# A seven-product block MLP for the second half of the tokens, and the sample's tokens in block 1

## The chip, the cores and the metric

The kernel runs on one core of a Trainium2 chip, as one program. The metric is the device time of one execution in microseconds, from runs on the chip. The engines of the core are named as the profile names them: PE (TensorE, matrix products), DVE (VectorE), ACT (ScalarE), POOL (GpSimd) and SP (SyncE, which here issues every DMA).

## The reference, cut to what matters

One layer of a streaming encoder is computed for a prompt of 2048 tokens and a sample of 32 tokens behind a cache of 128, with a model width of 1024:

```python
qa, ka, va, qb, kb, vb = split_proj(rmsnorm(h, g_attn), w_in)       # 1024 -> 3072
oa = differential attention, 4 heads, chunk-causal, T5 bias          # group A
ob = attention in a band of 9 chunks of 64, 8 heads, clipped bias    # group B
h = h + merge(oa, ob) @ w_out                                        # 1024 -> 1024
c = rmsnorm(h, g_mlp)
h = h + jnp.square(jax.nn.relu(c @ w_up)) @ w_down                   # 1024 -> 4096 -> 1024
h = h + jax.nn.sigmoid(h @ w_ple_gate) * (p @ w_ple_proj)
y = rmsnorm(h, g_final)
```

The outputs are y for prompt and sample and the new keys and values. All is in fp32.

## The kernel before

**Data.** Activations lie transposed: 128 partitions of channels, tokens along the free axis. The tokens are cut into four blocks, of 512, 512, 512 and 544 columns; the last block holds the 32 sample tokens. `SUBS` says in which column runs a block goes through a matrix product: one run of 512, and for the block of 544 two of 272. The residual h, the queries, keys, values and attention outputs are kept in DRAM between stages.

**Products.** Each fp32 operand is split into a high part, rounded to the matmul's format, and a low remainder. `split` (L167) has ACT make the high part and POOL (or DVE) the low part by a subtraction; POOL works in pieces of 256 columns (`pool_tt`, L148). `mm3` (L187) computes one product by three matmuls: high x high, high x low, low x high. A weight tile comes through `wunit` (L178): DMA of the raw tile (two buffers), high and low part (three buffers each).

**Stages.** `run` (L1105) prepares and projects blocks 0 and 1, then alternates attention over pairs of query tiles with projections of further blocks: group A's first half (`JA0`), group B's first half, group B's second half, group A's second half (`JA1`). The sample counts as pair 8, in the last tuple of `JA1` and `JB`; `caches` (L469) brings the cached keys and values into the scratch tensors ahead of block 3's projection. Then come output projection, MLP, gate and final norm. Blocks 0 and 1 go through the MLP one at a time, with two PSUM banks (`mm`), while the other six belong to attention. After that attention's banks go to a pool `md`: output projections of 2 and 3, gate and final of block 0, and then the MLP of blocks 2 and 3 together.

**The MLP** (`mlp`, L982) takes 256 of the 4096 hidden channels at a time: `mlp_up` (L922) multiplies two weight tiles by the normed activations (8 channel tiles, 24 matmuls a run), ACT applies relu and square, and the result is split; `mlp_down` (L950) multiplies it by two tiles of w_down for each of 8 output tiles (6 matmuls a run), and DVE adds each PSUM result to h in SBUF (L980). So the down sum over 4096 channels is made in SBUF, in 16 additions for each output.

**Order.** The order of instructions on each engine and of the DMAs on SP's queue is laid down when the program is compiled: a planner goes through a simulated time line, takes ready instructions by their place in the program, and hands out the buffers of the pools as they come free. `weave` and `weave2` interleave two stages by hand, `drain` runs one to its end. On the chip each engine and SP follows its list in order and waits by semaphores.

## Time and profile before

| | |
|---|---|
| runs (3) | 3239.21 us median, 3234.81 to 3240.3 |
| span of the profiled execution, first to last instruction | 3235.4 us |
| mean granted PE clock | 0.983 |
| PE / DVE / ACT / POOL busy | 3075.5 / 1568.3 / 1693.0 / 1715.2 us |
| matmuls | 17881 |
| DMA traffic | 489 MB, 151 GB/s over the span |

The profile gives no time of its own for the profiled execution beside the span; the difference of the median to the span is 3.8 us. Busy times overlap between engines, so they do not add up to the span. A PE time of one instruction overlaps that of the next; the pace of matmuls is read from their starts.

### The profile page before, as it was taken

What the parts mean: (1) busy time and instruction counts of PE and PEld (TensorE: products, weight loads), DVE (VectorE), ACT (ScalarE), POOL (GpSimd) and SP (SyncE); (2) the same over time, 40 slices, a digit from 0 to 9 for tenths busy, and PEclk for the clock granted to TensorE, in tenths of its full rate; (3) what the DMA queues carried; (4) which work ended last, traced back from release to release, by engine and by line L of the source; (5) the groups of instructions that cost most, each with busy time, mean ns of one, the idle gap of its engine ahead of it and who ended that gap; (6) DMA issues with size and microseconds to landing.
All of it is one profiled execution on the core that took longest, in us unless ns stands there. A gap on an engine that the chain in (4) does not pass through costs nothing.

```text
span 3235.4 us, 51443 instructions
## 1 busy us (share of the span) xinstructions
PE 3075.5 (95%) x17881; PEld 2690.7 (83%) x17881; DVE 1568.3 (48%) x3952; ACT 1693.0 (52%) x3717; POOL 1715.2 (53%) x2515
## 2 busy tenths in 40 slices
...
GB/s 233 156 256 247 227 246 212 197 255 212 209 235 226 207 144 135 157 162 140 183 136 153 148 114 121 130 131 271 146 100 46 47 46 46 46 46 46 50 94 89
DMA packets 519084, 489.02 MB, mean 151 GB/s; under 512 B 37884, under 2 KB 414016, under 8 KB 518824
## 3 DMA queue, kind: packets, MB, share of 16 engines
...
q8 instruction: 142, 2.33, 0.3%
q14 instruction: 118, 0.97, 0.1%
HBM read 379.06 MB, written 110.49 MB: 151 GB/s over the span
## 4 chain that ended last, share of the span: by engine, by line
PE 54%; DVE 5%; DMA 4%; ACT 2%; issue 1%; POOL 1%; SPq 0%; DVEq 0%; POOLq 0%; ACTq 0%
PE ups L191 7%; PE dps L191 7%; PE ups L192 7%; PE ups L193 7%; PE dps L192 7%; PE dps L193 7%; PE s L572 2%; PE gps L191 1%; PE gps L192 1%; PE gps L193 1%; DMA wr<-w_down 1%; PE tpp L644 1%; DVE e L609 1%; PE ob L771 1%; PE o L659 1%
## 5 line engine op out<-in xcount | busy, mean ns | idle before, releaser
L165 POOL TENSOR_TENSOR wl<-wr,wh 128x256 fp32r<-128x256 f32 x936 | 699.0, 780 | 473.4 <-ACT wh L170 448.6
L170 ACT ACTIVATE wh<-wr 128x1024 fp32r<-128x1024 f32 x338 | 357.2, 1058 | 611.4 <-PE dps L192 298.4
L980 DVE TENSOR_TENSOR h<-h,dps 128x512 f32<-128x512 f32 (+1 forms) x640 | 373.1, 585 | 578.4 <-PE dps L193 565.9
L155 POOL TENSOR_TENSOR wl<-wr,wh 128x256 fp32r<-128x256 f32 x416 | 304.3, 764 | 385.7 <-ACT wh L170 380.2
L191 PE MATMUL dps<-uh,wh 128*128 128x512 f32 (+1 forms) x1280 | 457.3, 357 | 16.9 <-DVE h L980 9.3
L191 PE MATMUL ups<-cH,wh 128*128 128x512 f32 (+1 forms) x1280 | 452.4, 354 | 10.0 <-ACT relu L945 8.1
L192 PE MATMUL ups<-cL,wh 128*128 128x512 f32 (+1 forms) x1280 | 451.5, 353 | 0.8 <-POOL cL L155 0.5
L193 PE MATMUL ups<-cH,wl 128*128 128x512 f32 (+1 forms) x1280 | 450.7, 352 | 0.0
L193 PE MATMUL dps<-uh,wl 128*128 128x512 f32 (+1 forms) x1280 | 449.7, 352 | 0.0
L192 PE MATMUL dps<-ul,wh 128*128 128x512 f32 (+1 forms) x1280 | 449.5, 351 | 0.0
L155 POOL TENSOR_TENSOR ul<-relu,uh 128x136 fp32r<-128x136 f32 (+1 forms) x320 | 200.5, 649 | 178.0 <-ACT uh L170 173.7
L191 PEld LDWEIGHTS dps<-uh,wh 128*128 128x128 f32 x1280 | 241.2, 188 | 52.2 <-DVE h L980 15.2
L191 PEld LDWEIGHTS ups<-cH,wh 128*128 128x128 f32 x1280 | 241.1, 189 | 43.6 <-ACT relu L945 8.9
L193 PEld LDWEIGHTS dps<-uh,wl 128*128 128x128 f32 x1280 | 240.8, 188 | 33.2 <-POOL wl L155 0.7
L192 PEld LDWEIGHTS ups<-cL,wh 128*128 128x128 f32 x1280 | 241.8, 189 | 31.5 <-POOL cL L155 0.8
L193 PEld LDWEIGHTS ups<-cH,wl 128*128 128x128 f32 x1280 | 241.4, 189 | 29.7
L192 PEld LDWEIGHTS dps<-ul,wh 128*128 128x128 f32 x1280 | 241.3, 189 | 26.0
L191 PE MATMUL qps<-aH,wh 128*128 128x512 f32 (+1 forms) x640 | 231.1, 361 | 10.0 <-ACT kr L433 3.4
L192 PE MATMUL qps<-aL,wh 128*128 128x512 f32 (+1 forms) x640 | 229.4, 358 | 0.0
L193 PE MATMUL qps<-aH,wl 128*128 128x512 f32 (+1 forms) x640 | 229.3, 358 | 0.0
L586 ACT ACTIVATE e<-s,nm 128x512 f32<-128x512 f32 (+3 forms) x256 | 155.2, 612 | 78.9 <-DVE nm L578 62.5
L572 PE MATMUL s<-ka,q 128*128 128x512 f32 (+3 forms) x768 | 184.0, 341 | 11.1 <-DMA q<-qS 3.7
(220 smaller groups left out, 7095.6 us busy)
## 6 DMA issues: line engine op xcount, KB each, us to landing
...
q<-qS SPq DMA_DIRECT2D x256, 128.0 KB, 4.1
...
```

Of the source, the lines that this page charges most:

```text
L155: nc.gpsimd.tensor_tensor(out[:, sl], a[:, sl], b[:, sl], op=op)
L165: nc.gpsimd.tensor_tensor(out[:, sl], a[:, sl], b[:, sl], op=op)
L170: nc.scalar.activation(hi, raw, AF.Copy)
L191: nc.tensor.matmul(ps, lh, rh, start=start and i == 0, stop=False)
L192: nc.tensor.matmul(ps, lh, rl, start=False, stop=False)
L193: nc.tensor.matmul(ps, ll, rh, start=False, stop=stop and i == n - 1)
L572: nc.tensor.matmul(s, q[:, m, hl, P * qi : P * qi + nr], kt[:, m, k0 - kb : k0 - kb + n], start=hl == 0, stop=hl == 1)
L586: nc.scalar.activation(dst, src, AF.Exp, bias=nmx, accum_out=z[:nr, m, bi : bi + 1])
L609: nc.vector.scalar_tensor_tensor(e[0][:nr, sl], e[0][:nr, sl], c[:nr, 0, bi : bi + 1], e[1][:nr, sl], op0=ALU.mult, op1=ALU.add)
L644: nc.tensor.transpose(tp[:kn, x, :nr], w[:nr, P * i : P * i + kn], self.ident[:nr, :nr])
L659: nc.tensor.matmul(oo, v[:kn, x, 0], pL[:kn, x, q0:nq], start=False, stop=False)
L980: nc.vector.tensor_tensor(hv, hv, ps, op=ALU.add)
```

## The change

**The sample** moves from block 3 to block 1. Block 1 becomes 544 columns in two runs of 272, block 3 becomes 512 in one. Scratch tensors keep the sample's columns behind block 1's (`T0`, `tcol`). The sample's attention becomes part of the second tuple of `JA0` and `JB`, and `caches` is called before all attention.

**The MLP of blocks 2 and 3** becomes two block products of 2 x 2, each by seven products in place of eight. The two token blocks are the two column halves of the right operand; its row halves are channels 0 to 511 and 512 to 1023 (up) and hidden channels 0 to 2047 and 2048 to 4095 (down).

- *Up* (`uphase`, `strassen`): for each of 16 groups of 256 hidden channels, `wquads` loads the weight's four quarters and makes four sums and differences (DVE). Each of seven products is 12 matmuls into one PSUM bank; ACT and DVE combine the products to four outputs; relu and square follow, and the result goes to DRAM (`uS`). The seven right operands are made once: `xnorm` norms, stores to DRAM (`cS`) and splits four of them beside block 0's gate, `xdiff` reads back and makes the three others after `final(0)`.
- *Down* (`dphase`): seven products in turn, each over the whole of a half's 2048 hidden channels in four PSUM banks, 192 matmuls. Both operands of each of 16 steps are formed and split as they are needed (`operand`); raw weights are loaded again for each product, activations once, through 24 buffers. After a product, DVE adds or subtracts its four banks into one or two quarters of h.

**Pools.** From the second half's output projection on, a new pool `tw` holds 5 raw weight buffers, 9 shared operand buffers and a ring of 14 tiles of 512 columns; all eight PSUM banks are one pool. The gate of block 1 uses the two banks `mm` as before.

```diff
 BLK = 544
 SUBS = {
     0: [(0, 512)],
-    1: [(0, 512)],
+    1: [(0, 272), (272, 272)],
     2: [(0, 512)],
-    3: [(0, 272), (272, 272)],
+    3: [(0, 512)],
 }
-BN = {0: 512, 1: 512, 2: 512, 3: 544}
+BN = {0: 512, 1: 544, 2: 512, 3: 512}
+T0 = {0: 0, 1: 512, 2: 1056, 3: 1568}
+TS = 1024
 HALVES = [(0, 1), (2, 3)]
...
-JA0 = [(0, 1), (2, 3)]
-JA1 = [(4, 5), (6, 7, 8)]
-JB = [(0, 1), (2, 3), (4, 5), (6, 7, 8)]
+JA0 = [(0, 1), (2, 3, 8)]
+JA1 = [(4, 5), (6, 7)]
+JB = [(0, 1), (2, 3, 8), (4, 5), (6, 7)]
...
         self.dma(raw, src)
-        hi = self.wp.tile([P] + shape, F32R, tag="wh", bufs=3, name="wh")
-        lo = self.wp.tile([P] + shape, F32R, tag="wl", bufs=3, name="wl")
+        th, tl, n = self.wtags
+        hi = self.wp.tile([P] + shape, F32R, tag=th, bufs=n, name="wh")
+        lo = self.wp.tile([P] + shape, F32R, tag=tl, bufs=n, name="wl")
         self.split(hi, lo, raw, hi_eng, lo_eng)
...
 
+    def quad(self, b, k):
+        return self.cS[:, k, 512 * (b - 2) : 512 * (b - 1)]
+
+    def tsplit(self, dst, src, lo_eng):
+        self.split(dst[:, 0], dst[:, 1], src, "act", lo_eng)
+
+    def xnorm(self, big, big2, t2, wk, out):
+        nc = self.nc
+        r = {}
+        for b in HALVES[1]:
+            r[b] = wk.tile([P, 512], F32, tag="r", bufs=2, name="rl")
+            self.dma(r[b], self.rS[:, T0[b] : T0[b] + 512])
+
+        def normed(b, k):
+            t = t2.tile([P, 512], F32, name="cn")
+            self.dma(t, self.hS[:, k, T0[b] : T0[b] + 512])
+            nc.vector.scalar_tensor_tensor(
+                t, t, self.g_mlp[:, k : k + 1], r[b], op0=ALU.mult, op1=ALU.mult
+            )
+            self.dma(self.quad(b, k), t)
+            return t
+
+        def x(pool, name):
+            out[name] = pool.tile([P, 4, 2, 512], F32R, tag="act", name="X" + name)
+            return out[name]
+
+        b11, b21 = x(big, "b11"), x(big, "b21")
+        for k in range(4):
+            for t, kk in ((b11, k), (b21, 4 + k)):
+                self.tsplit(t[:, k], normed(2, kk), "dve" if kk % 2 else "pool")
+            yield
+        b22, t3 = x(big2, "b22"), x(big2, "t3")
+        for k in range(4):
+            lo, hi = normed(3, k), normed(3, 4 + k)
+            self.tsplit(b22[:, k], hi, "pool")
+            nc.vector.tensor_tensor(lo, hi, lo, op=ALU.subtract)
+            self.tsplit(t3[:, k], lo, "dve")
+            yield
+
+    def xdiff(self, big, t2, out):
+        nc = self.nc
+        t1, tt2, t4 = [big.tile([P, 4, 2, 512], F32R, tag="act", name="X" + n) for n in ("t1", "t2", "t4")]
+        out.update(t1=t1, t2=tt2, t4=t4)
+        for k in range(4):
+            q = {}
+            for n, b, kk in (("12", 3, k), ("11", 2, k), ("22", 3, 4 + k), ("21", 2, 4 + k)):
+                q[n] = t2.tile([P, 512], F32, name="q" + n)
+                self.dma(q[n], self.quad(b, kk))
+            nc.vector.tensor_tensor(q["12"], q["12"], q["11"], op=ALU.subtract)
+            self.tsplit(t1[:, k], q["12"], "pool")
+            nc.vector.tensor_tensor(q["22"], q["22"], q["12"], op=ALU.subtract)
+            self.tsplit(tt2[:, k], q["22"], "dve")
+            nc.vector.tensor_tensor(q["21"], q["22"], q["21"], op=ALU.subtract)
+            self.tsplit(t4[:, k], q["21"], "pool")
+            yield
+
+    def wquads(self, W, c0, t2):
+        nc = self.nc
+        raw = []
+        for j in range(2):
+            r = self.rawp.tile([P, 4, 256], F32, bufs=self.nraw, name="wq")
+            self.dma(r, W[512 * j : 512 * j + 512, c0 : c0 + 256].rearrange("(k p) c -> p k c", p=P))
+            raw.append(r)
+        q = {"11": raw[0][:, :, :P], "12": raw[1][:, :, :P], "21": raw[0][:, :, P:], "22": raw[1][:, :, P:]}
+
+        def comb(n, x, y, op):
+            q[n] = t2.tile([P, 4, P], F32, name="w" + n)
+            nc.vector.tensor_tensor(q[n], q[x], q[y], op=op)
+
+        comb("s1", "21", "22", ALU.add)
+        comb("s2", "s1", "11", ALU.subtract)
+        comb("s3", "11", "21", ALU.subtract)
+        comb("s4", "12", "s2", ALU.subtract)
+        return q
+
+    def wsplit(self, src):
+        w = self.wp.tile([P, 2, 4, P], F32R, tag="wc", bufs=self.wtags[2], name="wc")
+        nc = self.nc
+        nc.scalar.activation(w[:, 0], src, AF.Copy)
+        for i in range(2):
+            sl = slice(2 * i, 2 * i + 2)
+            nc.gpsimd.tensor_tensor(w[:, 1, sl], src[:, sl], w[:, 0, sl].bitcast(F32), op=ALU.subtract)
+        return w
+
+    def prod(self, q, name, x, md):
+        w = self.wsplit(q[name])
+        ps = md.tile([P, 512], F32, tag="mm", name="xps")
+        self.mm3(ps, [(w[:, 0, k], w[:, 1, k], x[:, k, 0], x[:, k, 1]) for k in range(4)])
+        return ps
+
+    def strassen(self, W, g, X, t2, md):
+        nc = self.nc
+        q = self.wquads(W, 256 * g, t2)
+
+        def stage(n):
+            return t2.tile([P, 512], F32, name=n)
+
+        def comb(n, x, y, op=ALU.add, dst=None):
+            dst = stage(n) if dst is None else dst
+            nc.vector.tensor_tensor(dst, x, y, op=op)
+            return dst
+
+        u1 = stage("u1")
+        nc.scalar.activation(u1, self.prod(q, "11", X["b11"], md), AF.Copy)
+        c11 = comb("c11", u1, self.prod(q, "12", X["b21"], md))
+        p = self.prod(q, "s4", X["b22"], md)
+        c12 = stage("c12")
+        nc.scalar.activation(c12, p, AF.Copy)
+        p7 = self.prod(q, "s3", X["t3"], md)
+        p6 = self.prod(q, "s2", X["t2"], md)
+        u2 = comb("u2", u1, p6, dst=u1)
+        u3 = comb("u3", u2, p7)
+        p5 = self.prod(q, "s1", X["t1"], md)
+        u2 = comb("u4", u2, p5, dst=u2)
+        c22 = comb("c22", u3, p5)
+        c12 = comb("c12", c12, u2, dst=c12)
+        c21 = comb("c21", u3, self.prod(q, "22", X["t4"], md), ALU.subtract, dst=u3)
+        return (c11, c12), (c21, c22)
+
+    def uphase(self, X, t2, md):
+        nc, a = self.nc, self.a
+        for g in range(DFF // 256):
+            c = self.strassen(a["w_up"][0], g, X, t2, md)
+            for i in range(2):
+                for j in range(2):
+                    t = c[i][j]
+                    nc.scalar.activation(t, t, AF.Relu)
+                    nc.scalar.activation(t, t, AF.Square)
+                    self.dma(self.uS[:, 2 * g + i, 512 * j : 512 * j + 512], t)
+            yield
+
+    def dphase(self, h, up, t2, md):
+        nc, a = self.nc, self.a
+        Wd = a["w_down"][0]
+        u = {}
+
+        def urow(q, c):
+            if (q, c) not in u:
+                j, t = int(q[0]) - 1, int(q[1]) - 1
+                u[q, c] = up.tile([P, 2, 512], F32, tag="ud", name="u" + q)
+                self.dma(u[q, c], self.uS[:, 16 * j + 2 * c : 16 * j + 2 * c + 2, 512 * t : 512 * t + 512])
+            return u[q, c]
+
+        def wrow(q, c):
+            i, j = int(q[0]) - 1, int(q[1]) - 1
+            r = self.rawp.tile([P, 2, 512], F32, bufs=self.nraw, name="wd")
+            f = 16 * j + 2 * c
+            self.dma(r, Wd[P * f : P * f + 256, 512 * i : 512 * i + 512].rearrange("(k p) c -> p k c", p=P))
+            return r
+
+        def operand(src, k, op, lo):
+            if len(src) == 1:
+                v = src[0][:, k]
+            else:
+                v = t2.tile([P, 512], F32, name="dv")
+                nc.vector.tensor_tensor(v, src[0][:, k], src[1][:, k], op=op)
+            t = self.wp.tile([P, 2, 512], F32R, tag="wc", bufs=self.wtags[2], name="dc")
+            self.tsplit(t, v, lo)
+            return t
+
+        add, sub = ALU.add, ALU.subtract
+        plan = [
+            (("21", "22"), add, ("11",), add, (("21", add), ("22", sub))),
+            (("21", "11"), sub, ("11", "12"), add, (("22", add),)),
+            (("11", "22"), add, ("11", "22"), add, (("11", add), ("22", add))),
+            (("11",), add, ("12", "22"), sub, (("12", add), ("22", add))),
+            (("22",), add, ("21", "11"), sub, (("11", add), ("21", add))),
+            (("12", "22"), sub, ("21", "22"), add, (("11", add),)),
+            (("11", "12"), add, ("22",), add, (("11", sub), ("12", add))),
+        ]
+        for sq, so, tq, to, outs in plan:
+            ps = [md.tile([P, 512], F32, tag="mm", name="dp") for _ in range(4)]
+            for c in range(8):
+                ws = [wrow(q, c) for q in sq]
+                us = [urow(q, c) for q in tq]
+                for k in range(2):
+                    x = operand(us, k, to, "dve")
+                    w = operand(ws, k, so, "pool")
+                    for d in range(4):
+                        sl = slice(P * d, P * d + P)
+                        self.mm3(
+                            ps[d], [(w[:, 0, sl], w[:, 1, sl], x[:, 0], x[:, 1])],
+                            start=c + k == 0, stop=c == 7 and k == 1,
+                        )
+            for d in range(4):
+                for q, op in outs:
+                    i, t = int(q[0]) - 1, int(q[1]) - 1
+                    hv = h[2 + t][:, 4 * i + d, :512]
+                    nc.vector.tensor_tensor(hv, hv, ps[d], op=op)
+            yield
+
     def gfin(self, pool):
         self.gf = pool.tile([P, D], F32, name="gf")
         self.dma(self.gf, self.a["g_final"].unsqueeze(0).broadcast_to([P, D]))
 
     def gate(self, b, h, up, act, md):
         nc, a = self.nc, self.a
-        n, t0 = BN[b], 512 * b
+        n, t0 = BN[b], T0[b]
         Wg, Wp = a["w_ple_gate"][0], a["w_ple_proj"][0]
-        pT = [[up.tile([P, BLK], F32R, tag="u", name="pT") for _ in range(2)] for _ in range(2)]
+        pT = [[up.tile([P, up.aw], F32R, tag="u", name="pT") for _ in range(2)] for _ in range(2)]
         for i in range(2):
             for k in range(2):
                 self.dma(pT[i][k][:, :n], self.pS[:, i, k, t0 : t0 + n])
...
-            self.wp = opened(top, "wp", 3)
+            psx = ExitStack()
+            self.wp = opened(psx, "wp", 3)
             self.rawp = Rings((self.wp, "wr"))
-            mm = opened(top, "mm", MM, PSUM)
+            self.wtags = ("wh", "wl", 3)
+            mm = opened(psx, "mm", MM, PSUM)
             tp = mm
-            psx = ExitStack()
...
             psx.close()
-            wk = opened(top, "wk4", 1)
-            fk = opened(top, "fk4", 1)
-            self.nt = 8
-            self.rawp = Rings((self.wp, "wr"), (wk, "wr"))
+            self.wp = wp = opened(top, "tw", 1)
+            self.wtags, self.nraw = ("wc", "wc", 9), 5
+            self.rawp = Rings((wp, "wr"))
+            t2 = Sized(wp, 512, tag="t2", bufs=14)
+            md = opened(top, "md", 8, PSUM, "right")
+            t1x = ExitStack()
+            wk = Narrow(opened(t1x, "wk4", 1), t2)
+            fk = opened(t1x, "fk4", 1)
             self.gfin(fk)
-            md = opened(top, "md", 8 - MM, PSUM, "right")
-            act = Sized(opened(top, "acth", 4), BLK, True)
-            hh = opened(top, "hh", 2, side="right")
-            weave(self.outproj(2, wk, oa[2], md, acc[2]), self.oload(3, wk, act, oa), 1, 0, OW)
+            big = Sized(opened(t1x, "big", 5), 512, True)
+            weave(self.outproj(2, wk, oa[2], md, acc[2]), self.oload(3, wk, big, oa), 1, 0, OW)
+            uhx.close()
             g = self.outproj(3, wk, oa[3], md, acc[3])
             next(g)
-            self.colnorm(acc[2][0], 2, 1.0 / D, wk, mm, "mm", self.rS)
+            self.colnorm(acc[2][0], 2, 1.0 / D, wk, md, "mm", self.rS)
             drain(g)
-            h = hload(hh, BLK, 0)
-            g = self.gate(0, h, up, act, md)
+            b2x = ExitStack()
+            big2 = opened(b2x, "big2", 2, side="right")
+            h = hload(big, 512, 0, "act")
+            g = self.gate(0, h, t2, big, md)
             next(g)
-            self.colnorm(acc[3][0], 3, 1.0 / D, wk, mm, "mm", self.rS)
-            drain(g)
-            for b in HALVES[1]:
-                drain(self.cnorm(b, wk, act, cn))
-            f = self.final(0, h, up, fk, mm)
-            st = {b: (hload(hh, BLK, b),) + cn[b] for b in HALVES[1]}
-            m = self.mlp(HALVES[1], st, wk, up, mm, md)
-            next(m)
-            drain(f)
-            drain(m)
-            drain(self.gate(2, st[2][0], up, act, md))
-            g = self.gate(3, st[3][0], up, act, md)
-            f = self.final(2, st[2][0], up, fk, mm)
+            self.colnorm(acc[3][0], 3, 1.0 / D, wk, md, "mm", self.rS)
+            X = {}
+            weave(g, self.xnorm(big, big2, t2, wk, X), 1)
+            drain(self.final(0, h, t2, fk, md))
+            drain(self.xdiff(big, t2, X))
+            drain(self.uphase(X, t2, md))
+            b2x.close()
+            t1x.close()
+            hh = opened(top, "hh", 2)
+            h = {b: hload(hh, 512, b) for b in HALVES[1]}
+            udx = ExitStack()
+            drain(self.dphase(h, opened(udx, "ud", 24, side="right"), t2, md))
+            udx.close()
+            fk = opened(top, "fk5", 1)
+            self.gfin(fk)
+            act = Sized(opened(top, "acth", 4), 512, True)
+            drain(self.gate(2, h[2], t2, act, md))
```

The lines left out replace `512 * b` by `T0[b]`, test for block 1 in place of block 3, load the caches' columns for the sample's pair beside the prompt's, and widen the buffers of the first half's late stages to 544 columns.

132 lines of the change are left out of this document (78 added, 54 removed).

## The prediction

> **What bounds the kernel now.** I read the page first: the span, the busy shares, the chain that ended last.
>
> ```profile
> span 3235.4 us, 51443 instructions
> ...
> PE 3075.5 (95%) x17881; PEld 2690.7 (83%) x17881; DVE 1568.3 (48%) x3952; ACT 1693.0 (52%) x3717; POOL 1715.2 (53%) x2515
> ...
> PE 54%; DVE 5%; DMA 4%; ACT 2%; issue 1%; POOL 1%; SPq 0%; DVEq 0%; POOLq 0%; ACTq 0%
> ```
>
> PE is busy 95% and holds more than half of the chain; the other engines stand near half. Next came the table by stretches, cut where the work changes: projections and the first attention; block 0's and 1's MLP with the rest of the attention; gate and output projections; blocks 2 and 3's MLP; the last gates. Columns: length, busy time (instructions) of PE, PE's weight loads, DVE, ACT, POOL, granted clock, DMA share, GB/s.
>
> ```profile
> 0.00:1062.00 1062.00, 974.36 (x6136) 868.48 (x6137) 542.48 (x1765) 615.65 (x1466) 525.81 (x791) 0.97 0.76 224
> 1062.00:2090.00 1028.00, 1001.64 (x5193) 842.75 (x5192) 615.88 (x1488) 661.04 (x1490) 565.18 (x805) 1.00 0.52 146
> 2090.00:2372.00 282.00, 251.00 (x1271) 210.36 (x1269) 137.09 (x170) 131.01 (x220) 231.79 (x304) 0.96 0.55 171
> 2372.00:3100.00 728.00, 726.80 (x4507) 658.94 (x4508) 219.53 (x428) 212.98 (x380) 289.65 (x452) 1.00 0.17 53
> 3100.00:3235.40 135.40, 121.68 (x779) 110.18 (x777) 53.33 (x104) 72.35 (x164) 102.76 (x167) 0.96 0.29 95
> ```
>
> The stage the change rewrites is the fourth: PE 726.8 of 728.0 us at full clock, DVE, ACT and POOL at 30, 29 and 40%, DMA at 17%. A matmul taken away there is worth its whole pace, and there is room on the others for additions and subtractions. In the third stage POOL is at 82%.
>
> Matmuls overlap, so their cost is the distance between starts, not the duration. From PE's timeline, the first and last of 24 up-products on 512 columns and of 24 on 272:
>
> ```profile
> 2423.65 0.40 PE L191 MATMUL ups<-cH,wh 128*128 128x512 f32 x1
> ...
> 2429.03 0.40 PE L193 MATMUL ups<-cH,wl 128*128 128x512 f32 x1
> 2429.26 0.29 PE L191 MATMUL ups<-cH,wh 128*128 128x272 f32 x1
> ...
> 2432.15 0.29 PE L193 MATMUL ups<-cH,wl 128*128 128x272 f32 x1
> ```
>
> 23 steps in 5.38 us are 0.234 us at 512 columns; 23 steps in 2.89 us are 0.126 us at 272.
>
> **The main term.** Up and down each take 768 matmuls for a block of 512: 1536. Before, blocks 0, 1 and 2 have 1536 at 512 columns each and block 3 has 3072 at 272. After, block 1 has the 3072 at 272, block 0 its 1536, and blocks 2 and 3 together: up 16 groups x 7 products x 12 = 1344, down 7 x 8 x 2 x 4 x 3 = 1344, in all 2688 at 512. The 272s cancel; 4608 becomes 4224, so 384 matmuls go: 384 x 0.234 = 90 us. The gate rows below give 0.227 in their runs, so 87; I take **-88 us**. The sample's other work (projection, attention, gate) keeps its amount.
>
> **Do the new phases stay PE-bound?** Prices, from the groups by shape of 2400 to 3000 us:
>
> ```profile
> L980 DVE TENSOR_TENSOR h<-h,dps 128x272 f32<-128x272 f32 x202 | 88.5, 438 | 38.1 <-PE dps L193 31.7
> L980 DVE TENSOR_TENSOR h<-h,dps 128x512 f32<-128x512 f32 x101 | 69.5, 688 | 388.2 <-PE dps L193 388.2
> L170 ACT ACTIVATE uh<-relu 128x512 fp32r<-128x512 f32 x27 | 17.1, 632 | 0.9
> L945 ACT ACTIVATE relu<-ups 128x512 f32<-128x512 f32 x27 | 16.2, 599 | 108.1 <-PE ups L193 108.1
> L155 POOL TENSOR_TENSOR ul<-relu,uh 128x256 fp32r<-128x256 f32 x52 | 37.4, 741 | 85.6 <-ACT uh L170 85.6
> ```
>
> Up: a group's 84 matmuls take 84 x 0.23 = 19.3 us. Beside them DVE does 11 combinations (7.6 us), ACT 17 passes (10.6), POOL 14 pieces (10.4): all near half, with weights split more than a group ahead. Cost 0, hidden under PE; were the look-ahead gone, the wait would be one weight's split, about 2 us a group, 30 in all.
>
> Down: a step of 12 matmuls is 2.8 us. ACT makes two high parts (1.3), POOL two pieces (1.5), DVE the activation's low part and one combination, or two in three of the seven products: 1.4 or 2.1 us alone. But these DVE operations read both operands from SBUF, and so does POOL. DVE's timeline, then POOL's, then one row of the view by line (minimum/median/maximum ns):
>
> ```profile
> 2288.84 6.52 DVE L886 SCALAR_TENSOR_TENSOR tmp<-tmp,g_mlp_s,rl 128x512 f32<-128x512 f32 x6 [0.81 <-DMA rl<-rS]
> ...
> 2338.33 13.48 DVE L176 TENSOR_TENSOR cL<-tmp,cH 128x544 fp32r<-128x544 f32 x2 [5.21 <-ACT cH L170]
> ```
> ```profile
> 2291.32 2.33 POOL L155 TENSOR_TENSOR sig<-sm,sig 128x256 f32<-128x256 f32 x2
> 2293.61 4.39 POOL L155 TENSOR_TENSOR cL<-tmp,cH 128x256 fp32r<-128x256 f32 x4
> ...
> 2338.66 6.48 POOL L155 TENSOR_TENSOR cL<-tmp,cH 128x181 fp32r<-128x181 f32 x12
> 2345.10 5.49 POOL L165 TENSOR_TENSOR wl<-wr,wh 128x256 fp32r<-128x256 f32 x8
> ```
> ```profile
> L176 DVE TENSOR_TENSOR cL<-tmp,cH x16: 674/710/12852, 1035.9 to 2353.0; 128x512 fp32r<-128x512 f32 x12, 128x544 fp32r<-128x544 f32 x4
> ```
>
> Side by side they take turns: 1.09 us for each DVE operation and 1.10 to 1.17 for each POOL piece, against 0.67 and 0.74 alone. Once DVE stood 12.85 us while POOL ran twenty pieces. In a step with two combinations, two turns with POOL and one operation alone are 2 x 1.09 + 0.67 = 2.85 us against PE's 2.8, plus four or eight evictions of 0.69 a product. That is PE's own pace, with nine operand buffers (4.5 steps) as cushion: 0 if the cushion holds; without it 0.05 x 48 steps + 16 x 0.69 = 13 us. I take +5.
>
> The Trainium skill ("SBUF — State Buffer", section "Who interferes with whom") says more: the port is an exclusive lock, held for the whole instruction, and the loser blocks. By it a two-combination step would hold the port for 3 x 0.67 + 2 x 0.74 = 3.5 us; the rows of turns above show about 20% less than that sum, the 12.85 us row agrees with it. What this would give is a rival below.
>
> **What loads it.** SyncE issues all DMAs in an order written at compile time, and this order runs ahead wherever a buffer is free. From its queue and the DMA list:
>
> ```profile
> 2109.41 0.56 SPq L146 DMA_DIRECT2D h<-hS  x1
> 2119.97 18.88 SPq L146 DMA_DIRECT2D wr<-w_ple_gate  x4
> 2144.18 0.37 SPq L146 DMA_DIRECT2D wr<-w_out  x1
> ```
> ```profile
> h<-hS SPq DMA_DIRECT2D x4, 2048.0 KB, 10.6
> ```
>
> Block 0's h for the late gate is fetched before the weights of both output projections that precede its use. So at the start of the down phase I expect 24 activation tiles (12.6 MB) and up to two h tiles (4.2 MB) to be issued as their space comes free, ahead of weights. At 224 GB/s for a share of 0.76 (first stage) a full share is 295 GB/s: 16.8 MB are 57 us, against a cushion of 2.5 raw weight steps and 4.5 operand steps, about 26 us, and whatever goes out before the phase begins. 0 to 45 us; I take +5, since space frees in pieces over the last group's 19 us.
>
> **Block 1 in two halves, with two PSUM banks.** Its gate used 512 columns; now each of eight d has two runs of 272.
>
> ```profile
> 2123.64 0.39 PE L193 MATMUL gps<-hH,wl 128*128 128x512 f32 x1
> 2123.87 0.39 PE L191 MATMUL pps<-pT,wh 128*128 128x512 f32 x1
> ...
> 2126.16 0.50 PE L191 MATMUL gps<-hH,wh 128*128 128x512 f32 x1 [0.76 <-DVE sm L1025]
> ```
>
> The next gate product waits for Abs on ACT and min on DVE of the one before: 2126.16 - 2123.64 = 2.5 us, of which six matmuls cover 1.6. With 272 columns the passes shrink by about 0.45 us and the cover to 0.88: a wait of about 1.2 us sixteen times (19) for 0.9 eight times (7). +12, less what the next stage's matmuls fill: **+10** (0 to 20). Block 3's gate loses its halves, but had six banks.
>
> Block 1's down products: a pair of banks turns over every 6 x 0.126 = 0.75 us, and the eviction takes 0.44 plus two semaphores; before it was 1.40 against 0.69. The slack falls from 0.7 to 0.3 us less semaphores, while DVE is 60% busy with attention in that stage. Attention's own matmuls lie between, so **+8** (0 to 90, the rival below).
>
> **Moved work.** The sample's attention moves from the second to the first half of the pairs, the caches ahead of all attention, a fifth token tile into the opening preparation. In the first stage PE is idle 88 of 1062 us: other things pace it, so what was hidden under PE may show. Twelve small heads with some six ACT passes each, none over 0.44 us: 0 to 30; I take +5. SP's queue takes the caches' two dozen small transfers at that place; attention's key loads wait behind them, within the same bound.
>
> Between gate 0 and the new MLP, the differences need gate 0's two buffers, final's reads of h, and a round trip through DRAM; four of seven products need none of them (11 us a group, two groups possible). The third stage's 31 us of PE idle include the 12.85 us above, which may go. -10 to +20; +5. At the end, the last product's eight evictions stand before the first rows of gate 2's operand, about 3 us: +3.
>
> **Sum:** -88 + 5 (port) + 5 (loads) + 10 + 8 + 5 + 5 + 3 = **-47**. The profile's span 3235.4 becomes 3188; the runs' median is 3239.2, 3.8 above the span: **3192 us**. With every cost at its low end, -98: 3141.
>
> **Rivals.**
> - *All hidden*: all terms but gate 2's vanish, 3239 - 85 = 3154. For it: DVE, ACT and POOL at 30 to 40% in the old stage. Against: two banks with halves.
> - *The port is a lock*: each instruction keeps the other engine out for all its length, 3 x 0.67 + 2 x 0.74 = 3.5 us a step for PE's 2.8: 48 x 0.7 = 34 us in place of 5, 3221. For it the 12.85 us row; against, the turns of 1.09. (The rule of the Trainium skill above is this one.)
> - *The burst*: 45 in place of 5, 3232, PE standing in the first down product.
> - *Slower: block 1's evictions late.* 256 down half-products, each waiting for one foreign DVE operation (0.69 us, 60% of the time), are 256 x 0.69 x 0.6 = 106 us in place of 8, 3290. For it DVE's 60%; against, PE's order was laid with attention matmuls between. It decides from 55 us on, 0.21 us a half-product.
> - *It doesn't do what it says*: the planner puts PE's order so that the combinations stand between products; PE's matmul count falls by 384 and the stretch does not shrink: 3239.
>
> **How the numbers follow.** Forecast (3165 to 3212) 0.44; all hidden 0.2; lock 0.09; burst 0.08; evictions 0.13; no effect 0.06. Differences under 0.2% (6.5 us) can't be told from none. Faster: the first four, 0.81. Same 0.06, slower 0.13. The range leaves out most of the slower case and a little below: 3138 to 3250; the forecast's own is 3165 to 3212.
>
> **What would show it.** PE's matmul count falls by 384. Right: the up and down phases together take 2688 x 0.23 = 620 us with PE over 98% busy, and idle of PE before gps rises in block 1's gate. Wrong: PE in the down phase waits for DVE or POOL operands (lock), for DMA of raw weights at its start (burst), or for h in block 1's down products, that stage longer by over 55 us.

## The result, and the profile after

The changed kernel takes 3652.55 us (median of 4 runs, 3645.09 to 3658.39) against 3237.73 us for the kernel before on the same chip: a ratio of 1.1289, 95% interval [1.1266, 1.1311]. The forecast was 3192 us, 47 us faster; the change is 415 us slower. The page of the changed kernel, the lines that answer to those shown of before:

```profile
span 3656.6 us, 52371 instructions
...
PE 3190.0 (87%) x17497; PEld 2727.0 (75%) x17497; DVE 1790.1 (49%) x4218; ACT 1821.2 (50%) x3972; POOL 1839.8 (50%) x2595
...
PE 36%; DVE 6%; DMA 4%; issue 2%; POOL 2%; ACT 2%; SPq 0%; DVEq 0%; POOLq 0%; ACTq 0%
```

The 384 matmuls are gone (17881 to 17497), yet PE's share of the span falls from 95% to 87% and its share of the last chain from 54% to 36%. The table by stretches, cut where the work of this kernel changes (length, busy time and instructions of PE, PE's weight loads, DVE, ACT, POOL, granted clock, DMA share, GB/s):

```profile
0.00:1062.00 1062.00, 948.34 (x6028) 844.79 (x6028) 530.60 (x1853) 612.85 (x1526) 485.28 (x757) 0.95 0.75 216
1062.00:1170.00 108.00, 82.37 (x441) 66.13 (x440) 59.59 (x234) 72.74 (x158) 1.45 (x10) 0.83 0.40 104
1170.00:1680.00 510.00, 346.27 (x1568) 270.54 (x1568) 331.14 (x851) 324.99 (x884) 69.90 (x105) 0.74 0.40 106
1680.00:1757.00 77.00, 65.12 (x432) 60.68 (x433) 29.03 (x46) 27.63 (x39) 48.55 (x69) 0.90 0.67 208
1757.00:2544.00 787.00, 763.13 (x4619) 681.80 (x4618) 235.99 (x430) 292.65 (x461) 499.25 (x744) 0.99 0.34 104
2544.00:2812.00 268.00, 230.77 (x1180) 193.70 (x1179) 107.22 (x162) 120.70 (x225) 204.29 (x289) 0.92 0.55 171
2812.00:3150.00 338.00, 312.60 (x1348) 254.57 (x1348) 144.94 (x236) 161.05 (x307) 176.08 (x242) 0.96 0.37 124
3150.00:3510.00 360.00, 320.88 (x1355) 258.26 (x1356) 280.37 (x314) 141.41 (x243) 248.53 (x238) 0.95 0.59 202
3510.00:3656.60 146.60, 120.53 (x535) 96.55 (x533) 71.22 (x97) 67.20 (x133) 106.45 (x147) 0.91 0.25 83
```

The third row is the surprise, and it lies in work that the change hardly touches. For 510 us PE is busy 68%, at a granted clock of 0.74, and no other engine is near its limit. Which work is missing there is seen when the same stretch is asked for the up products of the MLP alone (the columns shown are PE, PE's weight loads, ACT, clock, DMA share, GB/s). Before, then after:

```profile
1062.00:1700.00 638.00, 238.00 (x960) 175.94 (x959) 23.34 (x40) 0.99 0.56 157
```
```profile
1062.00:1700.00 638.00, 0.00 (x0) 0.00 (x0) 0.00 (x0) 0.75 0.41 109
```

Before, block 0's MLP ran from 1062 us on and filled the gaps of attention A's second half. After, attention runs alone, and the MLP begins when it is over. PE's waits between 1170 and 1680 us of the changed kernel (engine and line that waits, what it waits for, us in total, times, longest) are attention's own chain, softmax on DVE and ACT, with nothing to put between:

```profile
PE tpp L666 <- DVE e L631: 71.4, 32, 4.4
PE s L594 <- ACT e L608: 44.0, 65, 2.3
PE s L594 <- DMA q<-qS: 15.8, 4, 14.3
```

No wait names what holds the MLP back, since the order was fixed at compile time. The compiled programs' address lists do (bytes in each partition). The first half's late buffers grow from one side of SBUF, attention A's pool from the other:

```
                                                         before   after
second output-projection operand (oq), end               127520   131616
last hidden-activation slot of blocks 0 and 1 (uq), end  128544   131616
attention A, second half: first tile (ba), begin         129248   130528
```

Before, 704 bytes lay between. The change widens the four output-projection operands and the tile of h, which lie below these ends, from 512 to 544 columns, 16384 to 17408 bytes each. (The activation slots had 544 columns, 2176 bytes, before as well; they are only pushed up.) The buffers now end 1088 bytes inside attention's pool, which begins 1280 bytes later, since the sample's keys have left it. A buffer that shares space with another waits until that one is done with, so the rest of the output projections, all of block 1's and the last quarter of block 0's that is woven with its loads, waits for all of attention A, and MLP 0 behind it. In the trace of the changed kernel the output projections stop at 1000.1 us; they go on right behind the last store of attention A's result (`os`), with their loads (`oraw`) on SP's queue and then their products on PE:

```profile
1677.78 0.33 SPq L165 DMA_DIRECT2D oT<-os  x1
1678.16 2.34 SPq L165 DMA_DIRECT2D oraw<-oT  x5
```
```profile
1687.14 0.79 PE L211 MATMUL ops<-oact,wh 128*128 128x512 f32 x1 [14.12 <-DVE hd L896]
```

What this costs and what is left without it, from the first matmul of each kind in PE's trace (us; "space mended" is the first experiment below, "tokens only" the third, "loads and order" the ninth):

| stage | before | after | space mended | tokens only | loads and order |
|---|---|---|---|---|---|
| start to block 0's MLP | 1062.0 | 1757.4 | 1092.1 | 1087.6 | 1085.3 |
| blocks 0 and 1's MLP, to gate 1 | 1034.6 | 786.9 | 1077.3 | 1075.7 | 1075.5 |
| gate 1 to blocks 2 and 3's first up product | 241.0 | 268.0 | 271.9 | 244.8 | 271.0 |
| their up and down products, to gate 2 | 759.1 | 695.3 | 694.2 | 725.1 | 673.2 |
| gate 2 to the end of the span | 138.7 | 149.0 | 148.2 | 135.2 | 134.6 |
| span | 3235.4 | 3656.6 | 3283.7 | 3268.4 | 3239.6 |

### The profile page after: what moved, and what is told of

Its sections match the earlier page's. It is cut to its first block, busy times and chain, and to the rows that moved or that the text cites. A ratio compares the mean times of both kernels' runs of the same rounds, so it can differ in the third digit from the quotient of the medians.

```text
span 3656.6 us, 52371 instructions
## 1 busy us (share of the span) xinstructions
PE 3190.0 (87%) x17497; PEld 2727.0 (75%) x17497; DVE 1790.1 (49%) x4218; ACT 1821.2 (50%) x3972; POOL 1839.8 (50%) x2595
## 4 chain that ended last, share of the span: by engine, by line
PE 36%; DVE 6%; DMA 4%; issue 2%; POOL 2%; ACT 2%; SPq 0%; DVEq 0%; POOLq 0%; ACTq 0%
PE dps L211 3%; PE ups L212 3%; PE ups L211 3%; PE ups L213 3%; PE dps L213 3%; PE dps L212 3%; PE xps L211 3%; PE xps L212 3%; PE xps L213 3%; DVE dv L1179 2%; PE dp L212 1%; PE dp L213 1%; PE dp L211 1%; DVE dc L195 1%; PE gps L211 1%
## 5 line engine op out<-in xcount | busy, mean ns | idle before, releaser
L184 POOL TENSOR_TENSOR wl<-wr,wh 128x256 fp32r<-128x256 f32 x808 | 595.9, 769 | 359.4 <-ACT wh L189 308.5
L1011 DVE TENSOR_TENSOR h<-h,dps 128x272 f32<-128x272 f32 (+1 forms) x384 | 199.8, 521 | 525.1 <-PE dps L213 524.8
L174 POOL TENSOR_TENSOR wl<-wr,wh 128x256 fp32r<-128x256 f32 x288 | 208.3, 755 | 164.0 <-ACT wh L189 158.2
L211 PE MATMUL dps<-uh,wh 128*128 128x272 f32 (+1 forms) x768 | 257.7, 336 | 16.0 <-DVE h L1011 13.2
L211 PE MATMUL ups<-cH,wh 128*128 128x272 f32 (+1 forms) x768 | 249.7, 325 | 5.6 <-ACT cH L189 5.6
L212 PE MATMUL ups<-cL,wh 128*128 128x272 f32 (+1 forms) x768 | 250.0, 326 | 0.8 <-POOL cL L174 0.8
L213 PE MATMUL ups<-cH,wl 128*128 128x272 f32 (+1 forms) x768 | 250.2, 326 | 0.0
L213 PE MATMUL dps<-uh,wl 128*128 128x272 f32 (+1 forms) x768 | 247.8, 323 | 0.0
L212 PE MATMUL dps<-ul,wh 128*128 128x272 f32 (+1 forms) x768 | 247.3, 322 | 0.0
L174 POOL TENSOR_TENSOR dc<-dv,dc 128x256 fp32r<-128x256 f32 x160 | 175.9, 1125 | 88.3 <-ACT dc L189 88.3
L211 PE MATMUL dp<-dc 128*128 128x512 f32 x448 | 176.2, 398 | 27.3 <-ACT dc L189 27.3
L212 PE MATMUL dp<-dc 128*128 128x512 f32 x448 | 179.2, 402 | 13.9 <-DVE dc L195 13.7
```

Source lines behind the costliest of these rows:

```text
L174: nc.gpsimd.tensor_tensor(out[:, sl], a[:, sl], b[:, sl], op=op)
L184: nc.gpsimd.tensor_tensor(out[:, sl], a[:, sl], b[:, sl], op=op)
L211: nc.tensor.matmul(ps, lh, rh, start=start and i == 0, stop=False)
L212: nc.tensor.matmul(ps, lh, rl, start=False, stop=False)
L213: nc.tensor.matmul(ps, ll, rh, start=False, stop=stop and i == n - 1)
L1011: nc.vector.tensor_tensor(hv, hv, ps, op=ALU.add)
```

## The experiments

Theory "space" says that the overlap of 1088 bytes makes nearly all of the slowdown; the rival says that the moved sample work and the new program order changed the planner's layout. All edits are to the changed kernel unless said otherwise.

**The norm pool behind the widened buffers.** The pool `fk`, which lay in front of them, is opened after them, so that they begin and end 4608 bytes lower; the end is at 127008. The pool `fk` itself then reaches into attention's pool, but it is needed only for the final norm of block 1.

```diff
-            fk = opened(sq_, "fk", 1)
-            self.gfin(fk)
 ...
             uq = Sized(opened(sq_, "uq", 8), BLK)
+            fk = opened(sq_, "fk", 1)
+            self.gfin(fk)
```

> The changed kernel whole, with one edit: the pool fk (final norm's g and small tiles, some 4.6 KB a partition) is opened behind uq and not ahead of oq, so that the buffers of output projection 1 and of MLP 0 and 1 end below the space of the second half of attention A. Theory space (in the changed kernel these buffers, widened to 544 columns, reach about 1 KB into that pool, so output projection 1 and both MLPs stand until attention is over): the MLP runs beside attention again and the 3653 us fall by 360 to 420, to 3235 to 3290. Rival order (the sample's place, the 272-column halves on two banks or the planner's priorities spoil that stage): no change beyond 30 us, 3620 to 3680.

Measured: 3284.2 us, ratio to before 1.0134 [1.0109, 1.0158]. The same computation is 368 us faster. The up products are back beside attention:

```profile
1062.00:1700.00 638.00, 232.87 (x1045) 180.11 (x1046) 22.59 (x42) 0.99 0.59 164
```

**The kernel before, with 1792 bytes taken away.** An unused tile in the pool below pushes the unwidened buffers up by as much; the second operand of the output projection then ends 64 bytes, and the last activation slot 1088 bytes, inside attention's pool.

```diff
             wk = opened(sq_, "wk", 1)
+            pad = wk.tile([P, 448], F32, name="pad")
+            nc.gpsimd.memset(pad[:, :8], 0.0)
```

> The kernel before, with one edit: a tile of 1792 bytes a partition that nothing uses but one small memset, in the pool wk, so that the same buffers reach 1088 bytes into attention A's second pool. All work and all widths are those of before. Theory space: output projection 1 and MLP 0 wait for attention's end, MLP 0 and 1 (1536 matmuls of 0.23 us each, twice) come after it: 3238 becomes 3560 to 3640. Rival order: the tile is nothing, 3230 to 3250.

Measured: 3604.3 us, ratio 1.1128 [1.1100, 1.1156]: 366 us from an unused tile. The row for up products is that of the changed kernel:

```profile
1062.00:1700.00 638.00, 0.00 (x0) 0.00 (x0) 0.00 (x0) 0.76 0.42 112
```

Space is thus shown from both sides. What remains is +46 us where -47 was forecast.

**The sample tokens' move alone**, with the space mended and blocks 2 and 3's MLP as before (the second half from `wk4` on is that of the kernel before, with 512 columns).

> One half of the change alone: the sample's tokens in block 1, its attention in the first half, the caches early, with the pool fk behind uq; blocks 2 and 3 keep the MLP of before, now at 512 columns each, with its pools. Theory space: no overlap, so near before: block 1's MLP costs 34 us more, block 3's 34 less, plus what two banks and the early attention cost: 3235 to 3275. Rival order: the slow stage comes with the sample's move, 3500 or more.

Measured: 3271.5 us, ratio 1.0103 [1.0080, 1.0126]. The move costs 34 us, and the seven-product MLP 13 more on top, where it should have gained. In the table the move is +25.6 ahead of MLP 0, +41.1 in blocks 0 and 1's MLP and -34.0 in blocks 2 and 3's (the halves of 272 columns change place), and little else.

The next four take one suspected cost each away from the space-mended kernel (3284.2 us).

**The caches' call further down**, between attention's two tuples:

```diff
-            self.caches(sg, tp)
 ...
                 for js in JA0:
+                    if 8 in js:
+                        self.caches(sg, tp)
                     self.attn_a(js, pool, ps_s, ps_t, ps_o)
```

> The changed kernel with its norm pool behind the widened buffers (3284.2 us), and beside that one thing: the cached keys and values are prepared between the first and the second step of attention A's first half, and no longer straight behind the preparation of p. Theory 'rings': what the moved sample tokens cost (+34 us with the old MLP) comes above all from the start, where the cache work sits in the same buffers as the preparation of p and the projection of block 0, so that the projection can't run ahead and TensorE waits (34 us of lost pace at 200 to 240 us, against 13 us before). Then MLP 0 starts 15 to 25 us earlier and the time is 3258 to 3270. Rival 'tokens': the cost is the sample tokens' own work that now lies ahead of the MLP (attention, a fifth token tile, 272-column halves in block 1's MLP); then the time stays within 6 us of 3284.

Measured: 3319.3 us, 35 us slower, by neither theory. The planner took the cache transposes at 203 us all the same, as before the edit, so the run did not test the stall; but MLP 0 starts at 1162.0 instead of 1092.1 us.

**The down phase's loads in the order of their use.**

```diff
+                with self.tc.issue_after(self.wd):   # the weight load in front
                     self.dma(u[q, c], ...)
 ...
+            if not h:                                # behind product 1's loads
+                with self.tc.issue_after(self.wd):
+                    h.update((b, hload(b)) for b in HALVES[1])
```

> The same base (3284.2 us); in the new down phase the loads of u are queued behind the weight loads that they belong to, and the two 2 MB loads of h behind those of the first product. Theory 'burst': TensorE's 41 us lost at the start of the down phase come from the h loads and 19 u tiles that go out ahead of the next weights; then 15 to 30 us go, and the time is 3254 to 3269. Rival 'space': the loss is that nothing of the down phase can be loaded before the up phase's buffers are free, and the whole bandwidth is needed either way; then the time is 3278 to 3290.

Measured: 3257.3 us, -27: theory "burst". SP's queue at the phase's start, in the space-mended kernel and then here (start, duration, what is issued, how many):

```profile
2769.58 1.27 SPq L165 DMA_DIRECT2D h<-hS  x2
...
2777.59 0.90 SPq L165 DMA_DIRECT2D u<-uS  x2
...
2789.22 24.49 SPq L165 DMA_DIRECT2D u<-uS  x19
2814.38 0.60 SPq L165 DMA_DIRECT2D gf<-g_final  x1
2815.89 1.56 SPq L165 DMA_DIRECT2D wd<-w_down  x2
```
```profile
2783.67 0.55 SPq L165 DMA_DIRECT2D u<-uS  x1
2784.27 3.93 SPq L165 DMA_DIRECT2D wd<-w_down  x2
2788.25 0.47 SPq L165 DMA_DIRECT2D u<-uS  x1
2788.76 4.18 SPq L165 DMA_DIRECT2D wd<-w_down  x2
2792.99 0.47 SPq L165 DMA_DIRECT2D u<-uS  x1
2793.51 2.45 SPq L165 DMA_DIRECT2D h<-hS  x2
```

Nineteen activation tiles, of which fifteen belong to the second and third product (the first has eight, and four had gone out), kept the next two weight tiles back until 2815.89 us; in order, the first product takes 51.2 us instead of 64.8. In the traces 19 of the 27 us lie behind the last up product. The others lie ahead of it, where the two programs have the same order of instructions on every engine: executions vary by some us, and those 8 us are no effect of the loads.

**The up phase's first group early.**

```diff
             drain(self.final(0, h, t2, fk, md))
+            q = self.first(X, t2, md)      # group 0: sums, all splits, products 11, 12, s4, s3
             drain(self.xdiff(big, t2, X))
```

> The same base (3284.2 us); the first group of the up phase has its weight sums and splits, and its first four products, issued ahead of the work that makes the three differences of activations (which only its last three products need). Theory 'order': TensorE's 26 us lost at the start of the up phase are the wait for weight sums queued behind block 0's end and the differences on VectorE and ScalarE; four products of 12 matmuls at 0.2285 us are 11 us of cover, and the time falls by 10 to 20 us, to 3264 to 3274. Rival 'loads': the wait is for the sixteen quarter tiles read back from memory, and the cover only moves it; then the time stays within 6 us of 3284.

Measured: 3281.2 us, -3, within the rival's 6 us. The products do run earlier, but the one gap becomes several. After two of them PE runs at half its pace. The ends of these two and of a third gap in PE's timeline (the wait ahead in brackets), and the time of the first two by windows of 4 to 5 us (the value before the DMA share is the granted clock):

```profile
2439.02 0.79 PE L211 MATMUL xps<-Xb,wc 128*128 128x512 f32 x1 [2.99 <-DVE sig L1275]
...
2442.18 0.63 PE L212 MATMUL xps<-Xb,wc 128*128 128x512 f32 x1
2442.60 0.63 PE L213 MATMUL xps<-Xb,wc 128*128 128x512 f32 x1
...
2453.51 0.80 PE L211 MATMUL xps<-Xb,wc 128*128 128x512 f32 x1 [4.43 <-ACT wc L1102]
...
2492.06 0.80 PE L211 MATMUL xps<-Xb,wc 128*128 128x512 f32 x1 [6.47 <-ACT wc L1102]
```
```profile
2439.00:2444.00 5.00, 4.98 (x12) 3.91 (x13) 4.39 (x4) 1.26 (x2) 4.98 (x5) 0.50 0.13 50
2444.00:2449.00 5.00, 3.82 (x18) 2.64 (x16) 4.08 (x9) 3.53 (x15) 0.00 (x0) 0.97 0.00 0
2449.00:2453.40 4.40, 0.08 (x1) 0.00 (x0) 4.31 (x15) 2.96 (x15) 0.00 (x0) 0.74 0.43 127
2453.40:2458.00 4.60, 4.49 (x11) 3.54 (x12) 4.60 (x11) 3.70 (x8) 4.47 (x5) 0.51 0.86 269
```

Matmuls are 0.42 us apart for 5 us after such a gap, against 0.228 else: twelve of them lose 12 x 0.19 = 2.3 us on top of the gap. That is not what took the gain, though: in the space-mended kernel the one long gap has its slow stretch too, and from 2420 to 2500 us the mean clock is 0.79 in both, with 31.5 us of waits there and 30.2 here. The gain is there at first and is lost at one place: the 97th matmul of the up phase comes 9.5 us earlier than in the space-mended kernel (2480.1 against 2489.6 us), then PE waits 6.47 us for weights of the next group, and the 109th comes only 1.3 us earlier (2492.1 against 2493.4). The cover moved the wait from the first group to the second. The rival had the size right but not the cause: it named the tiles read back from memory, and DVE, which makes the differences and the weight sums, waits for no load from 2440 to 2492 us.

**No sums in the down phase.** The sums and differences of operands are left out, the first of each pair is used alone, so the kernel no longer computes the down product.

```diff
-            if len(src) == 1:
+            if True:
                 v = src[0][:, k]
```

> The same base (3284.2 us); in the down phase the sums and differences of two weight or two activation tiles are left out, the first tile of each pair is used alone (both are still loaded), so the MLP's result isn't the reference's. This takes 160 two-operand instructions of 512 columns from VectorE, at the 0.98 to 1.03 us that they take there some 160 us of its 280 us in that phase. Theory 'hidden': away from the phase's start TensorE sets the pace and VectorE's lateness costs some 12 us; then the time falls by 5 to 15 us, to 3269 to 3279, and TensorE's matmuls stay at 0.2285 us. Rival 'port': the turns between VectorE and GpSimd set the down phase's pace; then it falls by more than 25 us.

Measured: 3254.7 us, -29.5, in the rival's range; in the traces 24 of it lie behind the last up product. The time of each product of the down phase, from its first matmul to the next product's, for the seventh to its own last (us; 192 matmuls at 0.2266 us are 43.5):

| product (operands that are sums) | 1 (w) | 2 (w, u) | 3 (w, u) | 4 (u) | 5 (u) | 6 (w, u) | 7 (w) |
|---|---|---|---|---|---|---|---|
| space mended | 64.8 | 53.3 | 48.3 | 45.8 | 43.5 | 48.7 | 43.3 |
| loads in order | 51.2 | 51.7 | 53.1 | 43.5 | 43.5 | 49.4 | 43.3 |
| no sums | 56.6 | 43.5 | 43.5 | 43.5 | 43.5 | 43.5 | 43.3 |

Without sums PE sets the pace in all but the first product. With them, a product with two sums takes 5 to 10 us more: 22 us over products 2 to 7, 24 with the loads in order. "Hidden" falls. The loss is not spread over the steps. Most steps of 12 matmuls keep their 2.72 us, and a few stand still for a remainder that comes late. PE's waits in products 2 to 7 of the space-mended kernel:

```profile
PE dp L212 <- DVE dc L195: 12.0, 10, 3.0
```

The longest stands in product 6, in a step of 7.42 us: 3.04 us of waiting, and then, from 1 us after the restart, 3.4 us at half pace. Over these 285 us the granted clock is 0.98, which adds 5 to 6 us to the 12.0. In the stretch from 2880 to 3100 us, with the sums and then without (busy us and mean ns of one behind the first bar, idle time and what ended it behind the second):

```profile
L195 DVE TENSOR_TENSOR dc<-dv,dc 128x512 fp32r<-128x512 f32 x70 | 70.8, 1015 | 11.6 <-ACT dc L189 11.5
L174 POOL TENSOR_TENSOR dc<-wd,dc 128x256 fp32r<-128x256 f32 x64 | 63.1, 1007 | 27.3 <-ACT dc L189 22.3 <-POOL dc L174 3.1 <-issue 1.9
```
```profile
L195 DVE TENSOR_TENSOR dc<-u,dc 128x512 fp32r<-128x512 f32 x78 | 65.3, 840 | 120.9 <-ACT dc L189 118.8 <-DMA wd<-w_down 1.9
L174 POOL TENSOR_TENSOR dc<-wd,dc 128x256 fp32r<-128x256 f32 x157 | 145.2, 944 | 69.1 <-ACT dc L189 69.1
```

DVE's remainders take 1.0 us beside the sums and 0.84 without, and the idle time ahead of them is 11.6 us against 120.9. The run takes the sums and their turns with GpSimd away together; that the turns are the cause is argued from three operations alone being 3 x 0.67 = 2.0 us of a step's 2.72, and not shown by itself. Nor is it a fixed price: in the ninth run, with the products in another order, product 3 takes 43.5 us, product 6 51.9 and product 2, now the last, 58.3. Its longest wait there is for a remainder that stands in GpSimd's queue behind twelve pieces of gate 2's operand:

```profile
PE dp L213 <- POOL dc L174: 8.7, 1, 8.7
```

What makes the difference between the other products was not tried.

**The caches in buffers of their own**, ahead of the preparation of p:

```diff
+                self.caches(wk, Rings((ps_t, "tp")))
                 self.prep_p(sg, wk, ps_t)
-            self.caches(sg, tp)
```

> The changed kernel with its norm pool behind the widened buffers (3284.2 us), and beside that one thing: the cached keys and values are prepared in buffers of their own (those of the setup stage, with two of its PSUM tiles), so that the preparation of p and the value projection no longer wait for them at 200 to 240 us. The run with the call moved further down had not tested this, since its trace shows the cache transposes at the same place (203 us). Theory 'rings': TensorE's 34 us of lost pace there fall to about 13 as before, and the time to 3255 to 3270. Rival 'order': the list scheduler, which fixes the order of all instructions at compile time, lays out the first 1060 us anew with every such edit, so that what is won at 200 us is not what comes out at MLP 0's start (the moved call cost 35 us, with nothing won or lost at 200 us); then the time lies anywhere in 3240 to 3330 and doesn't follow the 21 us.

Measured: 3301.6 us, 17 us slower than without the edit, though the stall is more than halved. The window from 200 to 240 us, of the kernel before, of the space-mended one, and here:

```profile
200.00:240.00 40.00, 32.38 (x182) 27.80 (x181) 7.44 (x14) 11.20 (x19) 19.77 (x29) 0.87 1.03 323
```
```profile
200.00:240.00 40.00, 14.13 (x68) 11.58 (x67) 7.34 (x13) 6.32 (x13) 0.14 (x1) 0.57 0.86 272
```
```profile
200.00:240.00 40.00, 28.61 (x203) 24.25 (x201) 7.65 (x16) 8.04 (x17) 9.52 (x14) 0.88 0.79 238
```

PE wins 14.5 us of work there, and MLP 0 starts at 1101.8 us, 10 us later. That is the rival "order".

**Down loads in order, and another order of the seven products** (5, 6, 1, 7, 3, 4, 2 of the list; the last one adds into quarter 22 alone).

> The base (3284.2 us) with the loads of the down phase in the order of their use (3257.3 us by itself), and its seven products in another order: first those that need the operands 21 and 11 of u, last the one that adds only into quarter 22, so that block 2's gate finds block 2's h complete one product earlier. Theory 'last product': TensorE's 10 us at the start of gate 2, a wait for the rounding of h behind the last additions, go, and the time is 3244 to 3252. Rival: gate 2 waits for its buffers, which the down phase holds to its end; then 3253 to 3262.

Measured: 3246.8 us, ratio 1.0024 [1.0009, 1.0039]: -10 by the order, -37 with the loads. The last stage falls from 148.2 to 134.6 us; a part of that comes back as the wait of 8.7 us in the last product, where gate 2's operand is now split. That leaves 0.24% above the kernel before, just over what can be told from none.

**All three edits together.**

> The three edits together: norm pool behind the widened buffers, caches in buffers of their own, down loads in order and the other order of products. If each is worth by itself what 'rings', 'burst' and 'last product' say, the sum from 3284 is -20 - 27 - 9 = 3228, and the time is 3215 to 3240, level with the kernel before or a little under it. If 'order' holds for the first 1060 us, it is 3215 to 3290, and differs from the run without the cache edit by whatever that edit did in its own run.

Measured: 3273.6 us, ratio 1.0101 [1.0083, 1.0118]. The caches' own buffers cost 27 us here and 17 us above; the two other mends are worth 28 here and 37 there. The two differ by about 10 us, which the intervals of these runs (5 to 8 us each way) can make, so they do not tell whether the mends add.

**Loads, order and the early first group** (the ninth and the sixth together).

> The run of down loads and product order (3246.8 us), with the first group's weight sums and first four products ahead of the activation differences as well (worth 3 us by itself). If the two add up, 3240 to 3247, which is 0.1 to 0.3% above the kernel before, or level with it; a result under 3236 would say that the early products are worth more once the phase behind them is not held up, and one above 3250 that the scheduler took back more than the three.

Measured: 3246.5 us, ratio 1.0022 [1.0012, 1.0033]: no different from the ninth.

**The kernel before, with only the call of the caches moved up** to where the changed kernel has it.

```diff
                 self.prep_p(sg, wk, ps_t)
+            self.caches(sg, tp)
 ...
             ppx.close()
-            self.caches(sg, tp)
```

> The kernel before, its sample tokens left in block 3 and its MLP untouched, with the one call that prepares the cached keys and values moved to where the changed kernel has it, straight behind the preparation of p. Theory 'place': the 34 us that the sample move cost come in the main from this call's place (TensorE's idle time at 200 to 240 us and what the schedule makes of it by MLP 0's start, 1062 us before and 1088 to 1092 with the move); then the time rises by 15 to 35 us, to 3255 to 3275, and MLP 0 starts at 1075 to 1095. Rival 'work': they come from the sample tokens' own work ahead of MLP 0; then the time stays within 6 us of the kernel before.

Measured: 3295.9 us, ratio 1.0168 [1.0144, 1.0192]: +56, more than theory "place" had, and more than the whole move of the tokens. MLP 0 starts at 1141.4 us, 79 later. The work moved is eight transposes, six splits and their transfers. So the place of this one call can cost more than the whole move, in a kernel where no token has moved. How much of the move's 34 us is the tokens' own work stays open.

**The sample's attention and the caches late again**, as steps of their own, the tokens still in block 1: on the space-mended kernel, with loads and order, and with the old MLP.

```diff
-JA0 = [(0, 1), (2, 3, 8)]
-JA1 = [(4, 5), (6, 7)]
-JB = [(0, 1), (2, 3, 8), (4, 5), (6, 7)]
+JA0 = [(0, 1), (2, 3)]
+JA1 = [(8,), (4, 5), (6, 7)]
+JB = [(0, 1), (2, 3), (8,), (4, 5), (6, 7)]
```

> The base (3284.2 us) with the cached keys and values prepared where the kernel before has them (behind the keys and values of block 2), and the sample's attention as a step of its own, first in the second half of group B and first in attention A's second half, so that it is still done before block 1's output projection. Theory 'place': the stall at 200 to 240 us goes and MLP 0 starts at 1062 to 1078 instead of 1092; the time is 3250 to 3270. Rival 'tokens': a step of 32 queries late in the chain delays block 1's output projection, and MLP 0 with it; then 3280 to 3320.

> The same late sample step with the down loads in order and the other order of products (3246.8 us without it). Theory 'place': 15 to 30 us less, 3217 to 3232, faster than the kernel before by 0.2 to 0.7%. Rival 'tokens': 3243 to 3285.

> The same late sample step with blocks 2 and 3's MLP left as before (3271.5 us with the early step, 34 us above the kernel before). Theory 'place': 3240 to 3256, so that moving the tokens costs 0 to 16 us once the caches stand where they were. Rival 'tokens': 3265 to 3305.

Measured: 3422.9, 3387.0 and 3420.2 us (ratios 1.0575, 1.0466, 1.0572, each within 0.003), 139 to 149 us slower than with the early step. Attention A's second half now holds a step that block 1's output projection needs, and group B's attention lies ahead of it in the chain: MLP 0 starts at 1344 to 1353 us. The first of the three, between 1060 and 1300 us:

```profile
1060.00:1300.00 240.00, 176.82 (x938) 145.31 (x939) 129.26 (x431) 141.16 (x341) 46.35 (x93) 0.81 0.58 150
```

It looks like the space overlap again, shorter: attention and, from 1226.7 us on, the late output projections (52.5 of PE's 176.82 us), no MLP, clock 0.81. That the step's place in the chain is the cause is read from the program's order; no run tried it apart from the caches' place, which moved with it. In this order, at least, the late step costs far more than the early one.

**The caches first of all, and second**, both on the kernel with loads and order.

```diff
+            self.caches(sg, tp)      # first
             drain(self.proj(HALVES[0], 0, acts, sg, mm, Rings((ps_t, "tp"))))
+            self.caches(sg, tp)      # or here: second
 ...
-            self.caches(sg, tp)      # behind the preparation of p
```

> The run of down loads and product order (3246.8 us), with the cached keys and values prepared ahead of the first projection, so that their turns in the shared buffers come before those of the preparation of p and of block 0's projections. Theory 'place': nothing queues behind the cache stores at 200 to 240 us, TensorE's busy time there is near the 32 of 40 us of the kernel before (14 with the call behind the preparation of p), and the time falls by 10 to 30 us to 3217 to 3237. Rival 'order': the schedule of the first 1060 us comes out anew, and the time is anywhere in 3230 to 3300 without following those us.

> The same with the call between the first projection and the setup stage. Theory 'place': as above, 3217 to 3237, within 8 us of the other. Rival 'order': the two differ by more than 10 us, although only the moment of the same small work differs.

Measured: 3248.5 us, ratio 1.0035 [1.0022, 1.0048], and 3299.8 us, ratio 1.0197 [1.0173, 1.0222]. PE's busy time at 200 to 240 us is 34.40 and 31.81 us, the stall is gone in both, and yet one equals the kernel with the stall and the other is 53 us slower. Theory "place", that the stall's us come back in the end, falls with this; "order" stands: MLP 0 starts at 1079.2 and at 1166.5 us, against 1085.3 with the call behind the preparation of p. Why the planner's layouts differ by that much stays open. No version was faster than the kernel before.

## Why the prediction was wrong

Its own sum, put into the five stages of the table (the 28 us that the halves of 272 columns move from block 3's MLP to block 1's are 3072 x 0.126 - 1536 x 0.234), against the space-mended kernel:

| stage | forecast | space mended | after |
|---|---|---|---|
| start to block 0's MLP | +5 (moved work) | +30 | +695 |
| blocks 0 and 1's MLP | +28 +8 (evictions) | +43 | -248 |
| gate 1 to the up products | +10 +5 | +31 | +27 |
| up and down | -88 -28 +5 (port) +5 (loads) | -65 | -64 |
| from gate 2 on | +3 | +9 | +10 |
| sum of the span | -47 | +48 | +421 |

**The step that failed** is one that has no term. The change's description on record says that the buffers of the first half's late stages are widened to 544 columns; the prediction costs block 1's two halves, its evictions and its gate, but never asks where the wider buffers lie. It took for granted that MLP 0 and 1 go on under attention A, which is what keeps PE at 1001.64 of 1028 us in the second row of before. That cover was 704 bytes wide. Its loss is 368 us, 7.8 times the forecast gain, and the range could not hold it. The rival on the slower side reached 3290 by late evictions in block 1's down products at 106 us; with the space mended that stage grew by 43 us, 28 of them the halves' own, so evictions and all else there cost 15. It did not come true either.

**Main term, -88.** The count is right to the instruction (384). The pace is 0.228 us where operands are there, and the old MLP at 512 columns takes 725.1 us for 3072 matmuls, 0.236 each: with PE always fed the new phases would take 2688 x 0.228 = 613 us, 112 less. They take 694. "PE over 98% busy" and 620 us, named as what would show it right, did not come.

**Loads, +5 within 0 to 45.** The rival "the burst" was the right picture, down to the h tiles and 24 activation tiles ahead of weights, and had 45 for its price; the fifth run took 19 to 27 us away with it. The prediction chose the low value because space would free in pieces over the last group. It does not: the tiles of u go out from 2777 us on, when the up phase ends, and all within 42 us.

**Port, +5.** The seventh run takes 24 us away behind the last up product, and the sums cost 22 us over products 2 to 7: nearer the 34 of the rival "the port is a lock" than the value chosen. As a price for every step neither holds: most steps with two sums keep 2.72 us, where the turns gave 2.85 and the lock 3.5, and a few wait up to 3.0 us. In those the cushion of nine operand buffers, which the low value rested on, did not hold. The Trainium skill ("SBUF — State Buffer", "Who interferes with whom") has the port as an exclusive lock, held for the whole instruction. Products 2 and 3 of the space-mended kernel do not agree with that, if an instruction holds it for as long as it takes alone:

```profile
2852.00:2954.00 102.00, 94.49 (x387) 73.57 (x386) 100.11 (x114) 37.72 (x65) 73.67 (x66) 0.97 0.57 183
```

Here 101 of DVE's 114 operations read two operands from SBUF; with POOL's 66 pieces that would be 101 x 0.67 + 66 x 0.74 = 116 us, in 102.

**Between gate 0 and the new MLP, +5.** From gate 0 to the first up product the space-mended kernel takes 69.8 us against 64.7, as forecast. The price comes one product later: in the ninth run's trace PE waits there at one blow:

```profile
PE xps L211 <- ACT wc L1102: 20.8, 1, 20.8
```

The forecast had counted on four products that need no differences as cover; in program order their weight sums stand behind block 0's end and the differences. When they were put in front, the wait moved to the weights of the second group. Nothing in the prediction had a price for that.

**Gate of block 1, +10.** From gate 1 to gate 0 the third run takes 181.9 us against 176.3, +5.6; the mechanism, waits of the next gate product for DVE's min, was right. From that run's waits of PE, gate 1 to gate 0:

```profile
PE gps L211 <- DVE sm L1247: 7.2, 7, 1.0
```

With the new MLP the same way takes 202.1 us. Those 20 us begin where the second half's pools replace the first's; no term had them, and they were not taken apart. **Gate 2, +3** measured about 10, and left the last stage with the other order of products.

**Moved work, +5 within 0 to 30.** +25.6 to +30.1, at the upper end of the range. That it lay there is luck: the prediction priced the sample's own work, and the runs show that the place of the caches' call alone moves MLP 0's start by +79 us in the kernel before, and by -6 and +81 with loads and order. How much the sample's work adds was not taken apart.
